# Turning the second 128 tokens inside the product ahead of it, eps on VectorE, and a closing product in quarters

## The chip, the cores and the metric

The kernel runs on one core of a Trainium2 chip. TensorE multiplies matrices, VectorE, ScalarE and POOL (GpSimd) work elementwise, and SP (SyncE) issues most of the DMAs. Each engine has its own queue and takes its instructions in the order in which they are written; it waits at the head of the queue until what the instruction needs is there. The metric is the device time of one execution in microseconds (us), as the median of several runs. Before the change it is 985.27 us (three runs, 982.47 to 986.35).

## The reference

A trunk of two layers works on 256 tokens of 1024 numbers each. A layer has three sub-layers, and each ends in a layer norm:

```python
for i in range(DEPTH):
    h = _layernorm(DN_ALPHA * h + 0.5 * _swiglu(h, ffn_w_in[i, 0], ffn_w_out[i, 0]), ln_g[i, 0], ln_b[i, 0])
    ...  # mix = _s5_mixer(h) in layer 0, _gmlp_mixer(h) in layer 1
    h = _layernorm(DN_ALPHA * h + mix, ln_g[i, 1], ln_b[i, 1])
    h = _layernorm(DN_ALPHA * h + 0.5 * _swiglu(h, ffn_w_in[i, 1], ffn_w_out[i, 1]), ln_g[i, 2], ln_b[i, 2])

def _swiglu(x, w_in, w_out):
    gate, up = jnp.split(x @ w_in, 2, axis=-1)
    return (jax.nn.silu(gate) * up) @ w_out
```

The SwiGLU has an inner width of 2816. The gMLP mixer starts with `gelu(x @ w_in + b_in)`, splits it into `u` and `v`, and normalises `v`. The norm is `(y - mean) * rsqrt(var + 1e-5) * g + b` over the 1024 numbers of a token.

## The kernel before

**Tiles.** The 256 tokens are two tiles of 128, `h[0]` and `h[1]` (t = 0 and 1), one token per partition. A product needs the tokens turned, features on partitions: `make_xt(t)` (L195) turns one tile with 8 small matmuls against the identity (`tps`, L187). ScalarE then writes the high part `xt` (L192) and VectorE the remainder (L193), in two halves of 512 columns. Every matrix product is done as three matmuls of such parts, high by high, high by low and low by high (`mm3`, L200: lines 201 to 203; `mm3t`, L205: lines 208 to 210).

**Weights.** `Stream` brings the weights in blocks of 128 x 2048 numbers. SP loads a block into one of three raw slots (L63), ScalarE casts it to `hi` and VectorE subtracts to `lo` (L88 and L89, or L96 and L97). At most five split blocks are alive. A block is split when `ws.tick(n)` is called at its place in the program, up to n blocks, and a raw slot is loaded anew once VectorE's subtraction has read it. So the places of the ticks set where the casts and subtractions stand in the queues of ScalarE and VectorE.

**A sub-layer boundary.** `close` (L276) ends a sub-layer: for t = 0 and then t = 1 it sums the last weight blocks into `acc`. Each tile's layer norm follows on VectorE: `r` (L239), statistics (L240, L247), two subtractions (L228), two final passes (L231). Its `rstd` comes from POOL in two instructions (`rstd_of`, L219): eps is added (L221), then the power -1/2 is taken (L222). Within the sums of t = 1, `close` turns `h[0]`. The next sub-layer then begins with t = 0: in an FFN with `step_in(0, 0)` and `step_in(1, 0)` (L361), the first two chunks of 256 inner columns, each a product of 24 matmuls of 512 columns; in the gMLP with `step_v` (L535) in the same way. Then `make_xt(1)` turns `h[1]`, and `step_in(0, 1)` and `step_in(1, 1)` follow for t = 1.

**What follows a step.** `in_act` (L354) applies silu on ScalarE and multiplies on VectorE (`g`, tile `sgg`, L358). In the steps for t = 1, `finish_g` (L343) transposes, after the first half of the product, the `g` that stand waiting (L348), at the first such place those of `step_in(0, 0)` and `step_in(1, 0)` together. Each step calls `ws.tick()` twice, in its middle and at its end. In the gMLP the additions of the bias to `v` (L547) and the norm of `v` follow the first two steps, and then eight heads of `u` (`step_u`, L550), 24 matmuls of 256 columns each.

**The boundaries here.** Three FFNs begin in this way (at about 341, 531 and 795 us of the profile), and the gMLP once (at 722 us). The first FFN and the S5 mixer begin in other ways.

**The end.** The last `close` sums the closing three blocks of the last FFN: for each t 18 matmuls for columns 0 to 511 and 18 for columns 512 to 1023 (`mm_out`, L441). The two halves of each normalised tile go out by one DMA each, from SP and from ScalarE's queue.

Of the kernel before, what the change touches and what calls it, by code (L numbers as in the profile page):

```python
# [9 lines left out]
F32 = mybir.dt.float32  # L10
# [3 lines left out]
ALU = mybir.AluOpType  # L14
PSUM = bass.MemoryType.PSUM

P = 128
D = 1024
KD = D // P
# [3 lines left out]
NCH = DFF // FC  # L23
# [131 lines left out]
def hybrid(ctx: ExitStack, tc: tile.TileContext, a: dict, out: bass.AP, subs=SUBS):  # L155
    nc = tc.nc
# [62 lines left out]
    def rstd_of(mv, eps):  # L219
        rstd = st_p.tile([P, 2], F32, tag="rstd", name="rstd")  # L220
        nc.gpsimd.tensor_scalar(rstd[:, 0:1], mv[:, 1:2], eps, 1.0, op0=ALU.add, op1=ALU.mult)  # L221
        nc.gpsimd.tensor_tensor(rstd[:, 1:2], rstd[:, 0:1], mhalf, op=ALU.pow)  # L222
        return rstd[:, 1:2]
# [51 lines left out]

    def close(li, si, acc, blocks, mm, gb, hscale, eps, last):  # L276

        order = [(n, j) for n in range(2) for j in range(len(blocks))]
        for t in range(2):
            for n, j in order:  # L280
                for kt in range(2):
                    mm(j, t, n, kt, acc[t][n])
                    if (t, n, j, kt) == (1, 1, len(blocks) - 2, 0) and not last:
# [7 lines left out]
            if t == 1 and not last:  # L291
                ws.tick(1)
            layernorm(t, acc[t], gb, hscale, eps, sums)
            if t == 1 and not last and next_kind[li, si] != "s5":
                ws.tick(1, 4)
            if last:
                for n in range(2):
                    s = slice(512 * n, 512 * n + 512)
                    (nc.sync, nc.scalar)[n].dma_start(out=out[0, P * t:P * t + P, s], in_=h[t][:, s])
# [33 lines left out]
    def ffn(ids, li, si, first, last):  # L333
        acc = [None, None]
        gts = {}
        pend = []
# [104 lines left out]
        def mm_out(c, t, n, kt, ps):  # L441
            gh, gl = (gts[c, kt][:, j, P * t:P * t + P] for j in range(2))
            wh, wl = ws.get(ids["out"][c])
            s = slice(D * kt + 512 * n, D * kt + 512 * n + 512)
            mm3(ps, gh, gl, wh[:, s], wl[:, s], c == 0 and kt == 0, c == NCH - 1 and kt == 1)
# [34 lines left out]
        close(li, si, acc, [ids["out"][c] for c in range(c0, NCH)], lambda j, t, n, kt, ps: mm_out(c0 + j, t, n, kt, ps),  # L480
# [48 lines left out]
    def gmlp(plan, par, pool, li, si, first, last):  # L529
# [5 lines left out]
        def step_v(c, t):  # L535
            ps = mm_p.tile([P, 512], F32, tag="mm", name="zps")
            in_mm(cols[c], t, ps, range(4))
            ws.tick()
            in_mm(cols[c], t, ps, range(4, KD))
            if t == 1:  # L540
                done(cols[c])
            ws.tick()
# [48 lines left out]
        pend = [step_v(0, 0), step_v(1, 0)]  # L591
        make_xt(1)
# [751 lines left out]
```

## Time and profile before

| | before |
|---|---|
| median of three runs | 985.27 us (982.47 to 986.35) |
| the profiled execution | 983.81 us, of which its span is 981.7 us |
| TensorE busy with matmuls | 948.4 us (97%) |
| VectorE busy | 650.1 us (66%) |
| ScalarE busy | 425.9 us (43%) |
| POOL busy | 165.6 us (17%) |
| mean granted clock of TensorE | 0.990 |
| chain of work that ended last | TensorE 66%, VectorE 18%, DMA 6%, POOL 3% |

The span is the time from the first to the last instruction of the profiled execution; the execution's own time is 2.1 us longer. Matmuls overlap, so their step from one start to the next is the measure of what they cost, not their duration. The chain follows the work that ended last back through the whole execution. In its second half it runs through TensorE alone, except at the sub-layer boundaries, where it passes through VectorE's norm.

### The profile page before, as it was taken

How to read it: one execution, taken by the hardware profiler on the slowest of the kernel's cores; microseconds unless marked ns; L12 is line 12 of the kernel's file. 1: busy time of each engine (PE TensorE's matmuls, PEld its weight loads, DVE VectorE, ACT ScalarE, POOL GpSimd, SP SyncE). 2: the span in 40 equal slices, each digit the busy share in tenths (PEclk: the TensorE clock that was granted, in tenths of full speed). 3: DMA queues.
4: the chain of work that ended last, by engine and by line, in shares of the span. 5: the costliest groups of instructions: out<-in, count | busy, mean ns of one | idle time of the engine just before them, and what ended most of it. 6: DMA issues, size and time to landing. Idle time of an engine off the chain costs nothing.

```text
span 981.7 us, 16616 instructions
## 1 busy us (share of the span) xinstructions
PE 948.4 (97%) x6988; PEld 860.6 (88%) x6988; DVE 650.1 (66%) x801; ACT 425.9 (43%) x504; POOL 165.6 (17%) x249
## 2 busy tenths in 40 slices
PE   7997999999999999999999999999999999999996
PEld 5996989978887789999997999999879879999995
DVE  5858999778797955455467644536588766453635
ACT  5554355644335445343423634344345445433430
POOL 1868811001572100000002000000011010000001
PEclk9998999999899999999999999999999999999998
DMA  8874796968645665746466674655447457555521
GB/s 278 224 223 162 265 280 220 289 214 285 221 146 183 189 209 179 237 133 233 152 200 216 211 272 154 204 182 179 164 155 275 129 173 265 163 194 192 168 90 43
DMA packets 133354, 195.10 MB, mean 199 GB/s; under 512 B 7120, under 2 KB 103936, under 8 KB 133280
## 3 DMA queue, kind: packets, MB, share of 16 engines
q1 hardware_dynamic: 128432, 182.34, 56.0%
q0 software_dynamic: 4560, 11.19, 3.9%
q8 instruction: 54, 0.88, 0.4%
q10 hardware_dynamic: 288, 0.52, 0.1%
q14 instruction: 20, 0.16, 0.0%
HBM read 184.07 MB, written 9.96 MB: 198 GB/s over the span
## 4 chain that ended last, share of the span: by engine, by line
PE 66%; DVE 18%; DMA 6%; POOL 3%; issue 3%; ACT 2%; SPq 0%; POOLq 0%; DVEq 0%; ACTq 0%
PE ips L210 11%; PE ips L209 11%; PE ips L208 11%; PE acc L201 7%; PE acc L202 7%; PE acc L203 7%; DVE lo L89 4%; DVE lo L97 4%; PE pps L1075 2%; DVE pq L639 1%; PE ips L203 1%; DMA raw<-in_ffn_w_out 1%; DVE prod L639 1%; ACT hi L96 1%; PE ips L201 1%
## 5 line engine op out<-in xcount | busy, mean ns | idle before, releaser
L210 PE MATMUL ips<-xt,lo 128*128 128x256 f32 x1184 | 335.5, 283 | 2.8 <-DVE lo L89 2.2
L208 PE MATMUL ips<-xt,hi 128*128 128x256 f32 x1184 | 335.4, 283 | 0.0
L209 PE MATMUL ips<-xt,hi 128*128 128x256 f32 x1184 | 335.0, 283 | 0.0
L89 DVE TENSOR_TENSOR lo<-raw,hi 128x2048 fp32r<-128x2048 f32 x107 | 242.9, 2292 | 11.1 <-ACT hi L88 10.7
L210 PEld LDWEIGHTS ips<-xt,lo 128*128 128x128 f32 x1184 | 227.1, 192 | 3.6 <-DVE lo L89 2.8
L208 PEld LDWEIGHTS ips<-xt,hi 128*128 128x128 f32 x1184 | 227.1, 192 | 1.5
L209 PEld LDWEIGHTS ips<-xt,hi 128*128 128x128 f32 x1184 | 227.1, 192 | 1.4
L88 ACT CAST hi<-raw 128x2048 fp32r<-128x2048 f32 x107 | 204.1, 1909 | 47.2 <-PE acc L203 26.6
L202 PE MATMUL acc<-lo,gt 128*128 128x512 f32 x352 | 138.5, 393 | 6.6 <-DVE lo L89 6.6
L398 DVE TENSOR_TENSOR sgg<-ips,sgg 128x256 f32<-128x256 f32 x74 | 31.3, 423 | 163.9 <-ACT sgg L397 163.8
L201 PE MATMUL acc<-hi,gt 128*128 128x512 f32 x352 | 138.7, 394 | 0.6 <-ACT gt L406 0.5
L203 PE MATMUL acc<-hi,gt 128*128 128x512 f32 x352 | 137.8, 391 | 0.0
L397 ACT ACTIVATE sgg<-ips 128x256 f32<-128x256 f32 x74 | 28.3, 383 | 214.2 <-PE ips L210 213.0
L221 POOL TENSOR_SCALAR rstd<-mv 128x1 f32<-128x1 f32 x14 | 10.4, 741 | 636.8 <-DVE mv L247 613.0
L97 DVE TENSOR_TENSOR lo<-raw,hi 128x2048 fp32r<-128x2048 f32 (+2 forms) x52 | 89.6, 1754 | 22.6 <-ACT hi L96 22.4
L202 PEld LDWEIGHTS acc<-lo,gt 128*128 128x128 f32 x352 | 66.7, 189 | 20.0 <-DVE lo L89 7.5
L201 PEld LDWEIGHTS acc<-hi,gt 128*128 128x128 f32 x352 | 66.7, 189 | 14.2 <-ACT gt L406 1.3
L203 PEld LDWEIGHTS acc<-hi,gt 128*128 128x128 f32 x352 | 66.5, 189 | 14.3 <-DVE gt L407 0.3
L96 ACT CAST hi<-raw 128x2048 fp32r<-128x2048 f32 (+2 forms) x52 | 74.5, 1482 | 3.6 <-DMA raw<-in_ffn_w_in 2.9
L407 DVE TENSOR_TENSOR gt<-sgg,gt 128x256 fp32r<-128x256 f32 x74 | 31.3, 423 | 59.5 <-ACT gt L406 59.5
L406 ACT CAST gt<-sgg 128x256 fp32r<-128x256 f32 x74 | 30.1, 406 | 68.1 <-DVE sgg L398 67.9
L201 PE MATMUL ips<-hi,xt 128*128 128x512 f32 x112 | 44.9, 401 | 3.8 <-ACT xt L192 2.3
(230 smaller groups left out, 1227.0 us busy)
## 6 DMA issues: line engine op xcount, KB each, us to landing
raw<-in_ffn_w_in SPq DMA_DIRECT2D x172, 512.0 KB, 5.8
raw<-in_ffn_w_out SPq DMA_DIRECT2D x44, 1024.0 KB, 5.2
raw<-in_g_w_in SPq DMA_DIRECT2D x8, 1024.0 KB, 5.8
rows<-w SPq DMA_DIRECT2D x8, 512.0 KB, 3.8
raw<-in_s_w_in SPq DMA_DIRECT2D x4, 1024.0 KB, 7.2
raw<-in_s_w_glu SPq DMA_DIRECT2D x4, 1024.0 KB, 5.2
w<-rows SPq DMA_DIRECT2D x8, 512.0 KB, 5.3
tc<-tc SPq DMA_DIRECT2D x16, 256.0 KB, 5.4
```

Of the source, the lines that this page charges most:

```text
L88: nc.scalar.copy(hi, raw)
L89: self.unfinished.append(lambda: nc.vector.tensor_tensor(lo, raw, hi.bitcast(F32), op=ALU.subtract))
L96: nc.scalar.copy(hi[:, s], raw[:, s])
L97: eng[p % len(eng)].tensor_tensor(lo[:, s], raw[:, s], hi[:, s].bitcast(F32), op=ALU.subtract)
L201: nc.tensor.matmul(ps, xh, wh, start=start, stop=False)
L202: nc.tensor.matmul(ps, xh, wl, start=False, stop=False)
L203: nc.tensor.matmul(ps, xl, wh, start=False, stop=stop)
L208: nc.tensor.matmul(ps, wh, xh, start=start, stop=False)
L209: nc.tensor.matmul(ps, wh, xl, start=False, stop=False)
L210: nc.tensor.matmul(ps, wl, xh, start=False, stop=stop)
L398: nc.vector.tensor_tensor(g, ps[:, 1], sg, op=ALU.mult)
L407: nc.vector.tensor_tensor(x[:, 1], g, x[:, 0].bitcast(F32), op=ALU.subtract)
```

## The change

The change has three parts.

**The turn.** `make_xt(1)` is called within `step_in(1, 0)` and `step_v(1, 0)`, after five of its eight k instead of after the whole step. The steps for (0, 0) no longer split a block (`split=0`); the first split after the boundary now stands behind the turn.

**eps.** `rstd_of` adds eps on VectorE; POOL keeps the power.

**The end.** `close_last` replaces `close` for the last FFN. For t = 1, columns 512 to 1023, the sum of the earlier blocks is closed early (`end` in `mm_out`) and added to `r` ahead of time. The last three blocks are summed for 256 columns at a time in tiles of their own (`ops`). Statistics are taken per 256 columns for t = 1, and the final pass and the output are in three parts, 512, 256 and 256 columns.

```diff
     def rstd_of(mv, eps):
         rstd = st_p.tile([P, 2], F32, tag="rstd", name="rstd")
-        nc.gpsimd.tensor_scalar(rstd[:, 0:1], mv[:, 1:2], eps, 1.0, op0=ALU.add, op1=ALU.mult)
+        nc.vector.tensor_scalar(rstd[:, 0:1], mv[:, 1:2], eps, 1.0, op0=ALU.add, op1=ALU.mult)
...
+    def close_last(acc, blocks, mm, gb, hscale, eps):
+        for t in range(2):
+            r = ln_p.tile([P, D], F32, tag="r", name="r", bufs=2)
+            parts = [(0, 512), (512, 512)] if t == 0 else [(0, 512), (512, 256), (768, 256)]
+            step = parts[-1][1]
+            st = st_p.tile([P, D // step, 6], F32, tag="bst", name="bst")
+            if t == 1:
+                s = slice(512, D)
+                nc.vector.scalar_tensor_tensor(r[:, s], in0=h[t][:, s], scalar=hscale, in1=acc[t][1], op0=ALU.mult, op1=ALU.add)
+            for i, (c, w) in enumerate(parts):
+                s, n = slice(c, c + w), c // 512
+                ps = acc[t][n] if w == 512 else mm_p.tile([P, 512], F32, tag="mm", name="ops")[:, 0:w]
+                for j in range(len(blocks)):
+                    for kt in range(2):
+                        mm(j, t, n, kt, ps, (c % 512, w), w < 512 and j == 0 and kt == 0)
...
+                x, scale = (h[t], hscale) if w == 512 else (r, 1.0)
+                nc.vector.scalar_tensor_tensor(r[:, s], in0=x[:, s], scalar=scale, in1=ps, op0=ALU.mult, op1=ALU.add)
+                for x in range(c, c + w, step):
+                    nc.vector.bn_stats(st[:, x // step], r[:, x:x + step])
...
+            for i, (c, w) in enumerate(parts):
+                s = slice(c, c + w)
+                nc.vector.scalar_tensor_tensor(h[t][:, s], in0=r[:, s], scalar=rstd, in1=b[:, s], op0=ALU.mult, op1=ALU.add)
+                (nc.sync, nc.scalar)[i % 2].dma_start(out=out[0, P * t:P * t + P, s], in_=h[t][:, s])
...
-        def step_in(c, t):
+        def step_in(c, t, mid=None, split=1):
             ps = mm_p.tile([P, 512], F32, tag="mm", name="ips")
-            in_mm(ids["in"][c], t, ps, range(4))
+            cut = 5 if mid else 4
+            in_mm(ids["in"][c], t, ps, range(cut))
+            if mid:
+                mid()
             if t:
                 finish_g()
-            ws.tick()
-            in_mm(ids["in"][c], t, ps, range(4, KD))
+            ws.tick(split)
+            in_mm(ids["in"][c], t, ps, range(cut, KD))
             in_act(c, t, ps)
             if t == 1:
                 done(ids["in"][c])
-            ws.tick()
+            ws.tick(split)
...
-            step_in(0, 0)
-            step_in(1, 0)
-            make_xt(1)
+            step_in(0, 0, split=0)
+            step_in(1, 0, lambda: make_xt(1))
             step_in(0, 1)
             step_in(1, 1)
...
-        pend = [step_v(0, 0), step_v(1, 0)]
-        make_xt(1)
+        pend = [step_v(0, 0, split=0), step_v(1, 0, lambda: make_xt(1))]
```

`step_v` is changed in the same way as `step_in`.

How this moves the instructions is shown at three places. A row names a line, an operation, what it writes and reads, and how often it stands there.

The first place is the beginning of the last FFN. This is a piece of the difference on TensorE. `tps` is the turn of `h[1]` (`h_95`); the weights `hi_7792` and `lo_7793` are the second half of `step_in(1, 0)`, `hi_7655` the beginning of `step_in(0, 1)`.

```order
@@ -4672,4 +4672,5 @@
 L202 MATMUL ips<-lo_7793,xt 128x512
 L203 MATMUL ips<-hi_7792,xt 128x512
+L187 MATMUL tps<-ident,h_95 128x128 x8
 L201 MATMUL ips<-hi_7792,xt 128x512
 L202 MATMUL ips<-lo_7793,xt 128x512
@@ -4681,5 +4682,4 @@
 L202 MATMUL ips<-lo_7793,xt 128x512
 L203 MATMUL ips<-hi_7792,xt 128x512
-L187 MATMUL tps<-ident,h_95 128x128 x8
 L201 MATMUL ips<-hi_7655,xt 128x512
 L202 MATMUL ips<-lo_7656,xt 128x512
```

The turn has moved up by nine matmuls. On VectorE there stood at the same place before the change (`lo` is a block split, `sgg` the `g` of a step, `xt` the turned tokens, `gt` the transposed `g`):

```order
L97 TENSOR_TENSOR lo_7793<-raw_7659,hi_7792 128x512 x4
L97 TENSOR_TENSOR lo_7819<-raw_7672,hi_7818 128x2048
L358 TENSOR_TENSOR sgg<-ips,sgg 128x256 x2
L193 TENSOR_TENSOR xt<-tps,xt 128x512 x2
L352 TENSOR_TENSOR gt<-tps,gt 128x128 x4
```

and now there stands on VectorE:

```order
L97 TENSOR_TENSOR lo_7793<-raw_7659,hi_7792 128x512 x4
L392 TENSOR_TENSOR sgg<-ips,sgg 128x256
L193 TENSOR_TENSOR xt<-tps,xt 128x512 x2
L97 TENSOR_TENSOR lo_7864<-raw_7672,hi_7863 128x2048
L392 TENSOR_TENSOR sgg<-ips,sgg 128x256
L386 TENSOR_TENSOR gt<-tps,gt 128x128 x4
```

The subtraction of the whole block (128x2048) has moved behind the turned tokens, and the second `g` behind that. ScalarE's cast of this block and its two silus have moved in the same way.

The second place is the beginning of the gMLP. VectorE before (`v` is the addition of the bias, BN_STATS the statistics of its norm):

```order
L97 TENSOR_TENSOR lo_7129<-raw_6998,hi_7128 128x512 x4
L97 TENSOR_TENSOR lo_7164<-raw_7010,hi_7163 128x2048
L193 TENSOR_TENSOR xt<-tps,xt 128x512 x2
L547 TENSOR_TENSOR v_7140<-zps,b_v 128x512 x2
L566 BN_STATS bst<-v_7140 128x6 x2
```

VectorE now:

```order
L97 TENSOR_TENSOR lo_7129<-raw_6998,hi_7128 128x512 x4
L193 TENSOR_TENSOR xt<-tps,xt 128x512 x2
L97 TENSOR_TENSOR lo_7206<-raw_7010,hi_7205 128x2048
L587 TENSOR_TENSOR v_7140<-zps,b_v 128x512 x2
L606 BN_STATS bst<-v_7140 128x6 x2
```

The block now stands between the turned tokens and the additions to `v`.

The third place is the end of the program, the norm of the last tile on VectorE. Before:

```order
L239 SCALAR_TENSOR_TENSOR r<-h_95,acc 128x512
L240 BN_STATS bst<-r 128x6
L239 SCALAR_TENSOR_TENSOR r<-h_95,acc 128x512
L240 BN_STATS bst<-r 128x6
L247 BN_AGGR mv<-bst 128x2
L228 SCALAR_TENSOR_TENSOR r<-r,mv,gam 128x512 x2
L231 SCALAR_TENSOR_TENSOR h_95<-r,rstd,bet 128x512 x2
```

Now:

```order
L286 SCALAR_TENSOR_TENSOR r<-h_95,acc 128x512
L298 SCALAR_TENSOR_TENSOR r<-h_95,acc 128x512
L300 BN_STATS bst<-r 128x6 x2
L298 SCALAR_TENSOR_TENSOR r<-r,ops 128x256
L300 BN_STATS bst<-r 128x6
L298 SCALAR_TENSOR_TENSOR r<-r,ops 128x256
L300 BN_STATS bst<-r 128x6
L302 BN_AGGR mv<-bst 128x2
L221 TENSOR_SCALAR rstd<-mv 128x1
L306 SCALAR_TENSOR_TENSOR r<-r,mv,gam 128x512 x2
L309 SCALAR_TENSOR_TENSOR h_95<-r,rstd,bet 128x512
L309 SCALAR_TENSOR_TENSOR h_95<-r,rstd,bet 128x256 x2
```

What waits for the last matmul is now 256 columns wide, and eps (`TENSOR_SCALAR rstd`) has come between the aggregation and the subtractions.

## Rows read from the trace of the kernel before

**Rows 1.** the page, part 1: busy us (share of the span), instructions; TensorE

```profile
PE 948.4 (97%) x6988; PEld 860.6 (88%) x6988; DVE 650.1 (66%) x801; ACT 425.9 (43%) x504; POOL 165.6 (17%) x249
```

**Rows 2.** TensorE's waits: who waited for whom, us in total, times, longest

```profile
PE ips L201 <- ACT xt L192: 2.3, 3, 0.8
...
PE tps L187 <- DVE h L231: 1.6, 2, 0.8
```

**Rows 3.** timeline, TensorE, last FFN's beginning: start, us, line, operation [idle before <- releaser]

```profile
792.60 0.39 PE L201 MATMUL ips<-hi,xt 128*128 128x512 f32 x1
...
793.45 0.40 PE L201 MATMUL ips<-hi,xt 128*128 128x512 f32 x1
...
795.50 1.03 PE L187 MATMUL tps<-ident,h 128*128 128x128 f32 x8
...
798.48 0.40 PE L201 MATMUL ips<-hi,xt 128*128 128x512 f32 x1
...
800.54 0.60 PE L348 MATMUL tps<-ident,sgg 128*128 128x128 f32 x4
```

**Rows 4.** timeline, TensorE, the gMLP's beginning, with the turn in `close` ahead

```profile
708.13 1.03 PE L187 MATMUL tps<-ident,h 128*128 128x128 f32 x8
...
709.23 0.39 PE L202 MATMUL acc<-lo,gt 128*128 128x512 f32 x1
...
722.14 1.03 PE L187 MATMUL tps<-ident,h 128*128 128x128 f32 x8
...
724.93 0.40 PE L201 MATMUL zps<-hi,xt 128*128 128x512 f32 x1
...
735.16 0.28 PE L208 MATMUL zps<-xt,hi 128*128 128x256 f32 x1
...
737.92 0.28 PE L210 MATMUL zps<-xt,lo 128*128 128x256 f32 x1
```

**Rows 5.** timeline, ScalarE, there

```profile
708.76 1.08 ACT L192 CAST xt<-tps 128x512 fp32r<-128x512 f32 x2 [9.78 <-PE tps L187]
```

**Rows 6.** timeline, VectorE, last FFN's beginning

```profile
792.13 4.69 DVE L97 TENSOR_TENSOR lo<-raw,hi 128x512 fp32r<-128x512 f32 x5
796.74 0.75 DVE L358 TENSOR_TENSOR sgg<-ips,sgg 128x256 f32<-128x256 f32 x2
```

**Rows 7.** the page, parts 5 and 6: groups (busy, mean ns), DMA issues (landing)

```profile
L89 DVE TENSOR_TENSOR lo<-raw,hi 128x2048 fp32r<-128x2048 f32 x107 | 242.9, 2292 | 11.1 <-ACT hi L88 10.7
...
L88 ACT CAST hi<-raw 128x2048 fp32r<-128x2048 f32 x107 | 204.1, 1909 | 47.2 <-PE acc L203 26.6
...
raw<-in_ffn_w_in SPq DMA_DIRECT2D x172, 512.0 KB, 5.8
```

**Rows 8.** timeline, VectorE, the gMLP's beginning

```profile
724.60 1.28 DVE L547 TENSOR_TENSOR v<-zps,b_v 128x512 f32<-128x512 f32 x2
...
740.53 0.68 DVE L547 TENSOR_TENSOR v<-zps,b_v 128x512 f32<-128x512 f32 x1
```

**Rows 9.** timeline, VectorE, the end of the program

```profile
973.52 0.69 DVE L239 SCALAR_TENSOR_TENSOR r<-h,acc 128x512 f32<-128x512 f32 x1 [1.85 <-PE acc L203]
...
974.97 0.21 DVE L247 BATCH_NORM_AGGREGATE mv<-bst 128x2 f32<-128x12 f32 x1
975.21 1.41 DVE L228 SCALAR_TENSOR_TENSOR r<-r,mv,gam 128x512 f32<-128x512 f32 x2
977.07 1.41 DVE L231 SCALAR_TENSOR_TENSOR h<-r,rstd,bet 128x512 f32<-128x512 f32 x2 [0.44 <-POOL rstd L222]
```

**Rows 10.** timeline, POOL, the end of the program

```profile
976.10 0.94 POOL L222 TENSOR_TENSOR rstd<-rstd,mhalf 128x1 f32<-128x1 f32 x1
```

**Rows 11.** groups of VectorE by line and shape: a narrow TENSOR_SCALAR

```profile
L645 DVE TENSOR_SCALAR n<-ch 128x32 f32<-128x32 f32 x1 | 0.2, 172 | 0.0
```

**Rows 12.** timeline, SP's DMA issues, last FFN's beginning

```profile
796.85 12.59 SPq L63 DMA_DIRECT2D raw<-in_ffn_w_in  x4
```

**Rows 13.** timeline, ScalarE, there

```profile
810.97 1.91 ACT L96 CAST hi<-raw 128x2048 fp32r<-128x2048 f32 x1
```

More of the change, by code (lines that the diff above doesn't have):

```diff
@@ L274, in new_acc @@
         return [acc_p.tile([P, 512], F32, tag="acc", name="acc") for _ in range(2)]
+    def close_last(acc, blocks, mm, gb, hscale, eps):
[13 more added lines that the diff above has]
+                        mm(j, t, n, kt, ps, (c % 512, w), w < 512 and j == 0 and kt == 0)
+                    if t == 0 and i == 0 and j < 2:
+                        ws.tick()
+                    if (t, i) == (1, len(parts) - 1):
+                        ws.done(blocks[j])
+                x, scale = (h[t], hscale) if w == 512 else (r, 1.0)
+                nc.vector.scalar_tensor_tensor(r[:, s], in0=x[:, s], scalar=scale, in1=ps, op0=ALU.mult, op1=ALU.add)
+                for x in range(c, c + w, step):
+                    nc.vector.bn_stats(st[:, x // step], r[:, x:x + step])
+            mv = st_p.tile([P, 2], F32, tag="mv", name="mv")
+            nc.vector.bn_aggr(mv, st)
+            rstd, (g, b) = rstd_of(mv, eps), gb
+            for n in range(2):
+                s = slice(512 * n, 512 * n + 512)
+                nc.vector.scalar_tensor_tensor(r[:, s], in0=r[:, s], scalar=mv[:, 0:1], in1=g[:, s], op0=ALU.subtract, op1=ALU.mult)
+            for i, (c, w) in enumerate(parts):
+                s = slice(c, c + w)
+                nc.vector.scalar_tensor_tensor(h[t][:, s], in0=r[:, s], scalar=rstd, in1=b[:, s], op0=ALU.mult, op1=ALU.add)
+                (nc.sync, nc.scalar)[i % 2].dma_start(out=out[0, P * t:P * t + P, s], in_=h[t][:, s])
@@ L276, in close @@
     def close(li, si, acc, blocks, mm, gb, hscale, eps, last):
+        if last:
+            return close_last(acc, blocks, mm, gb, hscale, eps)
         order = [(n, j) for n in range(2) for j in range(len(blocks))]
@@ L282, in close @@
                     mm(j, t, n, kt, acc[t][n])
-                    if (t, n, j, kt) == (1, 1, len(blocks) - 2, 0) and not last:
+                    if (t, n, j, kt) == (1, 1, len(blocks) - 2, 0):
                         make_xt(0, next_kind[li, si] == "s5")
@@ L290, in close @@
                     sums = layernorm_half(t, acc[t][0], 0, hscale)
-            if t == 1 and not last:
+            if t == 1:
                 ws.tick(1)
             layernorm(t, acc[t], gb, hscale, eps, sums)
-            if t == 1 and not last and next_kind[li, si] != "s5":
+            if t == 1 and next_kind[li, si] != "s5":
                 ws.tick(1, 4)
[L296 to L299, printed above, removed]
     def plan_ffn(li, fi, fine):
@@ L439, in start_in, with mm_out @@
             done(ids["in"][0])
-        def mm_out(c, t, n, kt, ps):
+        def mm_out(c, t, n, kt, ps, cols=(0, 512), start=False):
             gh, gl = (gts[c, kt][:, j, P * t:P * t + P] for j in range(2))
             wh, wl = ws.get(ids["out"][c])
-            s = slice(D * kt + 512 * n, D * kt + 512 * n + 512)
-            mm3(ps, gh, gl, wh[:, s], wl[:, s], c == 0 and kt == 0, c == NCH - 1 and kt == 1)
+            s = slice(D * kt + 512 * n + cols[0], D * kt + 512 * n + sum(cols))
+            end = NCH - 4 if last and (t, n) == (1, 1) and cols[1] == 512 else NCH - 1
+            mm3(ps, gh, gl, wh[:, s], wl[:, s], start or c == 0 and kt == 0, c == end and kt == 1)
         def step_out(c, t):
@@ L479, in ffn @@
         c0 = NCH - 3
-        close(li, si, acc, [ids["out"][c] for c in range(c0, NCH)], lambda j, t, n, kt, ps: mm_out(c0 + j, t, n, kt, ps),
+        close(li, si, acc, [ids["out"][c] for c in range(c0, NCH)], lambda j, *args: mm_out(c0 + j, *args),
               gb, 2 * ALPHA, 4 * EPS, last)
@@ L533, in gmlp, with step_v @@
         u = [pool.tile([P, SEQ], F32, name=f"u{h}") for h in range(HEADS)]
-        def step_v(c, t):
+        def step_v(c, t, mid=None, split=1):
             ps = mm_p.tile([P, 512], F32, tag="mm", name="zps")
-            in_mm(cols[c], t, ps, range(4))
-            ws.tick()
-            in_mm(cols[c], t, ps, range(4, KD))
+            cut = 5 if mid else 4
+            in_mm(cols[c], t, ps, range(cut))
+            if mid:
+                mid()
+            ws.tick(split)
+            in_mm(cols[c], t, ps, range(cut, KD))
             if t == 1:
                 done(cols[c])
-            ws.tick()
+            ws.tick(split)
             return c, t, ps
```

## The prediction

> **What bounds the kernel now.** Read the busy times of the engines first: TensorE's matmuls fill 97% of the 981.7 us span [rows 1]. VectorE and ScalarE have slack on average, so an edit on them is worth only what TensorE waits for, plus what lies behind the last matmul. The second view is therefore the list of TensorE's waits [rows 2]. Two of its lines belong to this change: three waits for the copies of the turned tokens (`ips L201 <- ACT xt`, 2.3 us in all) and two for the normalised tokens themselves (`tps L187 <- DVE h`, 1.6 us). The third view is the timeline of one sub-layer boundary, from which each of these gets its true size: a wait that is cut in pieces by a matmul in between shows only its first piece in the list.
>
> **1. The turn of tokens 128–255 (`make_xt(1)`), at three FFN boundaries.** Today TensorE finishes the product `step_in(1, 0)`, turns `h[1]` with 8 small matmuls, and then needs the result at once. From the first of the 8 at 795.50 to the fourth matmul of the next product at 798.48 [rows 3] pass 2.98 us. Nine matmuls take 2.05 us (793.45 to 795.50, [rows 3]), so one is 0.228 and three are 0.68; the turn costs 2.30 us at this place. Where `close` turns the other tokens inside a product, the trace has the price of a turn with cover: from its first matmul at 708.13 to the second one behind it at 709.23 [rows 4], 1.10 less one matmul, 0.87 us. The change makes every such turn a covered one: nine matmuls (2.05 us) follow it before the copies are wanted. The copies need 0.63 us until ScalarE starts (708.13 to 708.76) and 1.08 us for both halves [rows 4, 5], 1.71 in all; VectorE's part follows each by about 0.6. TensorE comes to them 0.87 + 2.05 = 2.92 us after the turn began, so the wait goes: 2.30 − 0.87 = 1.43 us.
>
> A second piece comes off in front of it. The matmuls of k = 4 take 0.85 us instead of 0.68 (792.60 to 793.45, [rows 3]), because their `lo` piece leaves VectorE only then (its run begins at 792.13, [rows 6]). That run hangs on the layer norm, which part 3 shortens by 0.22 us. So 0.17 us more, 1.60 in all.
>
> What the move pushes back is the block split that stood ahead of the turn. On ScalarE and VectorE the cast and the subtraction of 128x2048 elements (1.91 and 2.29 us, [rows 7]) now stand behind the copies of the turn, and the product `g` of `step_in(1, 0)`, which VectorE did directly after that of `step_in(0, 0)`, stands behind the subtraction. `finish_g` transposes this `g` twelve matmuls into the next product (800.54 now, [rows 3]). From the start of the turn: 1.71 + 1.91 + 2.29 + 0.42 (one of the two at 796.74, 0.75 together, [rows 6]) = 6.33 us. TensorE comes there after 0.87 + 21 × 0.228 = 5.66, and 0.18 more for the first pair, which is ready: 5.84. **A new wait of 0.5 us.** Its bounds: 0.2 if the row-to-row overlaps of some 0.1 us each hold here, 1.0 if cast or subtraction starts late by as much. I take 0.5, the plain sum of rows. Net 1.60 − 0.5 = 1.1 us, three times: **3.3 us**.
>
> **2. The same turn ahead of the gMLP product.** From 722.14 to the fourth matmul at 724.93 [rows 4] pass 2.79 us; less 0.68 and 0.87, 1.24, and with the 0.17 in front **1.4 us**. Here nothing transposes a `g`; the delayed split delays the additions to `v`. VectorE reaches the first of them 5.91 us (1.71 + 1.91 + 2.29) after a turn that starts at 722.14 − 2.05 − 0.17 = 719.92, so at 725.8 instead of 724.60 [rows 8]: 1.2 later. Its chain stays in that order until the last addition (740.53, 0.68 us, [rows 8]), then at about 741.5 to 742.2, as the norm between them gives 0.22 back. TensorE wants the bank that this frees for the fourth head: heads start at 735.16, are 24 matmuls of 0.12 us (23 of them between 735.16 and 737.92, [rows 4]), so at 735.16 − 1.4 + 3 × 2.88 = 742.4. That is cover of 0.2 us; if it is gone, it costs some tenths.
>
> **3. eps on VectorE instead of POOL.** In each of 14 norms VectorE waits for `rstd` (0.44 us at the last, [rows 9]), since POOL first adds eps and then takes the power (0.94 us, [rows 10]). Now VectorE adds, and POOL's power runs under the two subtractions: 0.94 us against 977.07 − 975.21 − 0.44 = 1.42 us [rows 9]. The wait goes and a one-column instruction comes. The trace has none on VectorE. Its bounds are 0.17 us (32 columns, [rows 11]) and 0.24 us, the step from the 12-column aggregation to what waits for it (974.97 to 975.21, [rows 9]); zero is excluded, since the addition must end before POOL starts and VectorE is in order. I take 0.22, so 0.22 us gained per norm. [...] On the path this lies only where TensorE waits for `h`: the two turns of [rows 2], **0.4 us** together, and the tail. Elsewhere matmuls hide it.
>
> **4. The tail.** The last 512 columns are summed as 18 + 18 matmuls of 256 columns instead of 18 of 512. TensorE: 36 × 0.12 against 18 × 0.228 is 0.22 later, about the same until the result can be read. VectorE then has half the columns for sum and statistics: from 973.52 to 974.97 [rows 9] are 1.45 us, two instructions of 0.42 with 0.03 between are 0.90, so −0.55; the earlier part's additional instructions run while TensorE still computes. eps +0.22, the wait for `rstd` −0.44, the last pass in three parts +0.1 (one more fixed part, estimated from 0.42 for 256 columns against 1.41 for two of 512, [rows 6, 9]). Sum: 0.22 − 0.55 + 0.22 − 0.44 + 0.1 = **−0.45 us**. What follows (981.7 − 978.5 = 3.2 us for the last output DMA and its end) I leave as it is, although the last transfer is half as large; at best that is some tenths more. [...]
>
> **Sum.** 3.3 + 1.4 + 0.4 + 0.45 = 5.6 us. Against the profiled execution's own 983.8 us this gives 978.2. The three timed runs (982.5, 985.3, 986.4) and it have their middle at 984.5, a little under the stated median of 985.27; from there 978.9, said as 979.0.
>
> **Rivals.** *The wait moves instead of going.* The transposes of `g` wait for a split that was hidden until now. If ScalarE's cast or VectorE's subtraction comes a microsecond late, each FFN boundary nets 0.1 instead of 1.1, and the time is 984.5 − 2.6 = 981.9. For it: 0.5 us of this wait stands in the sum already. Against it: both blocks have landed long before, and both engines are idle there.
>
> [...]
>
> *Slower: the weight stream falls behind.* SP's queue keeps its order, but the raw slot of the moved split is refilled only when its subtraction is over. Now that is 796.8 [rows 12]; then 793.3 + 5.9 = 799.2, while TensorE is 1.1 ahead: 3.4 us later against TensorE. A stream without slack would hand this over at all four boundaries, 13.6 − 5.6 = 8 us, 992.5. Against it: the load issued at 796.85 lands in 5.8 us [rows 7] and is first cast at 810.97 [rows 13]. That is 8.3 us of slack, of which 4.9 remain; it decides from a landing of 10.7 us on.
>
> **How the numbers follow.** Forecast 0.56, moved wait 0.25, hardly any new wait 0.15, slower 0.04. A measurement of this kernel can tell 0.5% (4.9 us, 980.3) from no change. Single runs of before lie 4 us apart, so I let a quarter of the forecast fall short of that line, and nearly all of the moved wait: faster 0.61, same 0.34, slower 0.05. The range goes from the better case with a low base (976) to the moved wait with a high one (983).
>
> **What would show it.** Right: no `ACT xt` or `DVE xt` wait among TensorE's longest after 330 us; in its place three of about 0.5 us of the transposes of `sgg` for VectorE; 9 matmuls between turn and next product without a gap; no idle time before the `rstd` pass; about 0.9 us between the last matmul's result and the aggregation. Wrong: waits over 1 us at the `sgg` transposes or at the heads of the gMLP, VectorE's one-column instruction over 0.44 us, or TensorE waiting for `lo` within the two chunks that follow a boundary.

## The result and the profile after

The changed kernel takes 977.83 us as the median of 13 runs (975.61 to 982.53), beside 984.23 for 13 runs of the kernel before (981.69 to 986.35). The ratio is 0.9936 with a 95% interval of 0.9921 to 0.9952: 6.3 us, or 0.64%, faster. The profiled execution took 976.03 us, its span is 974.3.

The engines' busy times (page, part 1; columns as in [rows 1]) have hardly changed, and so the gain is waiting time:

```profile
PE 948.1 (97%) x7006; PEld 863.4 (89%) x7006; DVE 652.0 (67%) x820; ACT 425.4 (44%) x504; POOL 157.2 (16%) x235
```

TensorE's waits (us in total, times, longest). Before, the list had for the gMLP, beside the lines of [rows 2],

```profile
PE zps L201 <- DVE xt L193: 1.0, 1, 1.0
```

After, neither this line nor that of `ACT xt` is on the list any more; the wait for `h` of [rows 2] fell from 1.6 to 0.6, and the new wait for the second `g` has come:

```profile
PE tps L382 <- DVE sgg L392: 0.6, 3, 0.2
PE tps L187 <- DVE h L231: 0.6, 2, 0.3
```

The beginning of the last FFN after, on TensorE, which answers to [rows 3] (start, us, line, operation, idle before and its releaser):

```profile
787.61 1.03 PE L187 MATMUL tps<-ident,h 128*128 128x128 f32 x8
788.40 0.48 PE L201 MATMUL ips<-hi,xt 128*128 128x512 f32 x1
788.72 0.40 PE L202 MATMUL ips<-lo,xt 128*128 128x512 f32 x1
...
790.54 0.39 PE L201 MATMUL ips<-hi,xt 128*128 128x512 f32 x1
...
793.27 0.38 PE L382 MATMUL tps<-ident,sgg 128*128 128x128 f32 x2
793.84 0.44 PE L382 MATMUL tps<-ident,sgg 128*128 128x128 f32 x2 [0.20 <-DVE sgg L392]
...
794.36 0.39 PE L202 MATMUL ips<-lo,xt 128*128 128x512 f32 x1
```

The turn at 787.61 is followed by nine matmuls without a gap, and the next product starts at 790.54 without a wait. The transposes of the first `g` start at 793.27, those of the second only at 793.84. From the first transpose to the second matmul behind them pass 1.09 us; before, the four together took 0.67, from 800.54 [rows 3] to the second matmul behind them,

```profile
801.21 0.39 PE L202 MATMUL ips<-lo,xt 128*128 128x512 f32 x1
```

So the new wait costs 0.42, of which the list shows 0.20. VectorE after shows why:

```profile
788.40 0.42 DVE L392 TENSOR_TENSOR sgg<-ips,sgg 128x256 f32<-128x256 f32 x1
788.87 1.29 DVE L193 TENSOR_TENSOR xt<-tps,xt 128x512 fp32r<-128x512 f32 x2
791.16 2.29 DVE L97 TENSOR_TENSOR lo<-raw,hi 128x2048 fp32r<-128x2048 f32 x1 [1.01 <-ACT hi L96]
793.37 0.42 DVE L392 TENSOR_TENSOR sgg<-ips,sgg 128x256 f32<-128x256 f32 x1
```

The second `g` (793.37) stands behind the block (791.16), as the order said, and is done at 793.79, 0.05 before TensorE goes on.

**Where the time went, place by place.** Take the same matmul in both traces and subtract its starts; where this shift grows, the change gains. Over the first FFN boundary, for example, these are the two matmuls before the change

```profile
335.10 0.39 PE L203 MATMUL ips<-hi,xt 128*128 128x512 f32 x1
...
518.22 0.48 PE L201 MATMUL acc<-hi,gt 128*128 128x512 f32 x1
```

and the same two after it:

```profile
333.22 0.39 PE L203 MATMUL ips<-hi,xt 128*128 128x512 f32 x1
...
515.15 0.48 PE L201 MATMUL acc<-hi,gt 128*128 128x512 f32 x1
```

The shift grows from 1.88 to 3.07 us, so this boundary gains 1.19. In the same way for all places, and for the experiments below (us gained against before; the pairs of matmuls start before the change at 213.09 and 219.21, 318.00 and 335.10, 335.10 and 518.22, 526.04 and 700.19, 716.06 and 782.29, 791.01 and 955.05; the end runs from 968.10 to the end of the span):

| kernel | turn that waits for `h`, first / second | FFN 1 / 2 / 3 | gMLP | end | sum |
|---|---|---|---|---|---|
| predicted | 0.2 / 0.2 | 1.1 / 1.1 / 1.1 | 1.4 | 0.45 | 5.6 |
| changed kernel | 0.48 / 0.53 | 1.19 / 1.16 / 1.14 | 1.42 | 0.64 | 6.56 |
| changed, second time | 0.47 / 0.52 | 1.19 / 1.14 / 1.18 | 1.42 | 0.64 | 6.56 |
| turn alone | −0.01 / 0.03 | 1.05 / 0.96 / 0.96 | 1.21 | 0.01 | 4.21 |
| eps alone | 0.48 / 0.52 | 0.47 / 0.46 / 0.47 | 0.19 | 0.49 | 3.08 |
| end alone | −0.01 / 0.04 | 0.03 / −0.06 / 0.00 | 0.00 | 0.16 | 0.16 |
| split left ahead | 0.47 / 0.50 | 0.83 / 0.73 / 0.82 | 0.49 | 0.63 | 4.47 |
| split behind, turn not moved (FFN) | 0.46 / 0.52 | 0.79 / 0.77 / 0.77 | 1.41 | 0.63 | 5.35 |
| split one product later | 0.49 / 0.53 | 0.80 / 0.78 / 0.77 | 1.42 | 0.63 | 5.42 |
| turn after four k | 0.58 / 0.52 | 1.62 / 1.54 / 1.60 | 1.42 | 0.64 | 7.92 |
| transposes later | 0.46 / 0.53 | 1.62 / 1.55 / 1.60 | 1.43 | 0.64 | 7.83 |
| transposes later, second time | 1.14 / 0.48 | 1.62 / 1.54 / 1.60 | 1.43 | 0.62 | 8.43 |

The two spans differ by 7.45 us, 0.89 more than this sum. The rest lies in the first 213 us and in the S5 mixer, where the change touches nothing that TensorE waits for. When the changed kernel ran a second time, the sum was again 6.56, while the rest was −2.94 us. So a single span tells a part of this size poorly, and the places behind 318 us tell it to some hundredths. The first turn is less safe: in the last row it gained 1.14 instead of 0.46 to 0.58. There the list of waits has `h` once, with 0.3 us, where the changed kernel's two traces have it twice, with 0.6 in all; the mean granted clock from 205 to 320 us was 0.96 in that trace and 0.97 in the changed kernel's two. Why the first turn didn't wait there is not shown.

### The profile page after: what moved, and what is told of

Same layout as the page of the kernel before. It is cut to its first block, busy times and chain, and to the rows that moved or that the text cites. A ratio compares the mean times of both kernels' runs of the same rounds, so it can differ in the third digit from the quotient of the medians.

```text
span 974.3 us, 16658 instructions
## 1 busy us (share of the span) xinstructions
PE 948.1 (97%) x7006; PEld 863.4 (89%) x7006; DVE 652.0 (67%) x820; ACT 425.4 (44%) x504; POOL 157.2 (16%) x235
## 4 chain that ended last, share of the span: by engine, by line
PE 64%; DVE 1%; ACT 1%; issue 0%; DVEq 0%
PE ips L210 11%; PE ips L209 11%; PE ips L208 11%; PE acc L201 7%; PE acc L202 7%; PE acc L203 7%; PE ips L203 2%; PE ips L201 2%; PE ips L202 2%; PE zps L210 1%; PE zps L209 1%; PE zps L208 1%; PE zps L202 1%; PE zps L203 1%; PE zps L201 1%; DVE lo L97 1%
## 5 line engine op out<-in xcount | busy, mean ns | idle before, releaser
L202 PE MATMUL acc<-lo,gt 128*128 128x512 f32 x346 | 136.2, 394 | 4.4 <-DVE lo L89 4.4
L201 PE MATMUL acc<-hi,gt 128*128 128x512 f32 x346 | 136.2, 394 | 0.0
L203 PE MATMUL acc<-hi,gt 128*128 128x512 f32 x346 | 135.2, 391 | 0.0
L222 POOL TENSOR_TENSOR rstd<-rstd,mhalf 128x1 f32<-128x1 f32 x14 | 13.3, 951 | 640.8 <-DVE rstd L221 640.8
L203 PEld LDWEIGHTS acc<-hi,gt 128*128 128x128 f32 x346 | 65.4, 189 | 14.0 <-DVE gt L444 0.2
L201 PEld LDWEIGHTS acc<-hi,gt 128*128 128x128 f32 x346 | 65.4, 189 | 13.0 <-ACT gt L443 0.4
```

What stands on the lines that cost most here:

```text
L201: nc.tensor.matmul(ps, xh, wh, start=start, stop=False)
L202: nc.tensor.matmul(ps, xh, wl, start=False, stop=False)
L203: nc.tensor.matmul(ps, xl, wh, start=False, stop=stop)
```

## The experiments

**The three parts apart.** The theory was that the parts add up, each worth what the start-to-start times say. The first kernel has the turn (and the splits that it takes along) alone:

```diff
-            step_in(0, 0)
-            step_in(1, 0)
-            make_xt(1)
+            step_in(0, 0, split=0)
+            step_in(1, 0, lambda: make_xt(1))
```

> Only the turn of the tokens is moved (with the splits that it takes along); eps stays on POOL and the end stays as before. Theory (the parts add up, and each is worth what the start-to-start times of TensorE show): at each FFN boundary the stall of 1.43 us goes and a wait of 0.42 us for the second g comes, the gMLP boundary gains 1.27, so 3 x 1.01 + 1.27 = 4.3 us, about 980 from a base of 984.2; the pause of 0.17 us in k = 4 stays, since the layer norm is as slow as before. Rival (eps is what lets the turn pay, because the copies hang on the norm): under 3 us, and a wait of the copies of the turned tokens stays in TensorE's list. Rival (the wait moves): about 1 us, with waits of 1 us and more at the transposes of g.

Measured: 980.34 us (11 runs, 975.38 to 981.79), ratio 0.9952 (0.9935 to 0.9969); in the trace 4.21 us. No wait of the copies is left; two lines of TensorE's waits:

```profile
PE tps L187 <- DVE h L231: 1.6, 2, 0.8
...
PE tps L348 <- DVE sgg L358: 0.5, 3, 0.2
```

The theory holds, and the turn doesn't need the faster norm. The wait for `h` stands as in [rows 2]; the next kernel, with eps alone, must take it.

```diff
-        nc.gpsimd.tensor_scalar(rstd[:, 0:1], mv[:, 1:2], eps, 1.0, op0=ALU.add, op1=ALU.mult)
+        nc.vector.tensor_scalar(rstd[:, 0:1], mv[:, 1:2], eps, 1.0, op0=ALU.add, op1=ALU.mult)
```

> Only eps moves to VectorE. Theory (start to start): a norm is 0.49 us shorter, because the wait for rstd cost 0.56 from start to start and not the 0.44 that the trace calls idle, and because the one-column instruction holds VectorE up by 0.07 and not 0.22. On the path at the two turns that wait for h (0.98), in the tail (0.49) and in the four pauses of 0.17 us in k = 4 after a boundary: 2.1 us, about 982. Rival (the prediction's sizes, 0.22 per norm): 0.44 + 0.22 + 4 x 0.17 = 1.3 us. Rival (hidden everywhere but in the tail): 0.5 us.

Measured: 980.36 us (12 runs, 978.24 to 984.86), ratio 0.9971 (0.9956 to 0.9986); in the trace 3.08 us, more than any of the cases expected. The two turns and the end came out as the theory said (0.48, 0.52, 0.49). What it missed is 0.47 at each FFN boundary instead of 0.17. TensorE there:

```profile
791.88 1.03 PE L187 MATMUL tps<-ident,h 128*128 128x128 f32 x8
793.39 0.47 PE L201 MATMUL ips<-hi,xt 128*128 128x512 f32 x1 [0.48 <-DVE sgg L358]
...
794.56 0.40 PE L201 MATMUL ips<-hi,xt 128*128 128x512 f32 x1
```

and VectorE:

```profile
790.62 2.29 DVE L97 TENSOR_TENSOR lo<-raw,hi 128x2048 fp32r<-128x2048 f32 x1
792.82 0.75 DVE L358 TENSOR_TENSOR sgg<-ips,sgg 128x256 f32<-128x256 f32 x2
```

With the norm 0.49 shorter, the stall at the turn is 0.30 shorter too (794.56 − 791.88 = 2.68, against 2.98 before [rows 3]), and its releaser is now named as the first `g`: that is done at 792.82 + 0.42 = 793.24, and the matmul starts 0.15 later. Before, the first of the two `g` at 796.74 [rows 6] was done at 797.16, and the matmul started at 797.30, also 0.14 later, though the list put that wait down to ScalarE's copies. These are TensorE's rows of before, and VectorE's copies of the turned tokens behind its two `g`:

```profile
797.30 0.47 PE L201 MATMUL ips<-hi,xt 128*128 128x512 f32 x1 [0.77 <-ACT xt L192]
...
798.14 0.50 PE L203 MATMUL ips<-hi,xt 128*128 128x512 f32 x1
```

```profile
797.41 1.28 DVE L193 TENSOR_TENSOR xt<-tps,xt 128x512 fp32r<-128x512 f32 x2
```

So the stall that the change removes hung on VectorE's queue. The next product is taken to need the PSUM tile of the first one (the fourth tile before it in a pool of four), which is free when the first `g` has read it, and that `g` stood behind the block. Which tile it takes is read from the code; what the traces show is the same lag in both kernels. And this is only the first piece of the stall: the third matmul (798.14) waits once more, for VectorE's copy of the first half of the turned tokens, the remainder. This copy ends at 797.41 + 0.68 = 798.09, 0.05 before the matmul, and stands behind the block and both `g`: it began 0.69 after ScalarE's part was done (796.72), where 0.03 is enough in the split-behind kernel below. This was a new theory, and the next experiments are made for it.

The third part alone:

```diff
+        if last:
+            return close_last(acc, blocks, mm, gb, hscale, eps)
```

> Only the closing product is changed; eps stays on POOL. Theory: TensorE 0.22 later, 0.53 less between result and aggregation, 0.06 more for the aggregation of four parts, 0.13 more for a third final pass, the last store as slow as before: 0.1 to 0.2 us faster in the trace from the first matmul of the last 512 columns to the end, nothing that the times can tell. The wait for rstd of 0.44 us must still stand there. [...] Rival (the additional 18 matmuls cost more than the halves give): 0.2 us slower.

Measured: 985.86 us (12 runs, 982.71 to 990.46), ratio 1.0017 (0.9998 to 1.0036), which tells nothing from no change; in the trace 0.16 us. VectorE's last instructions:

```profile
973.37 0.42 DVE L298 SCALAR_TENSOR_TENSOR r<-r,ops 128x256 f32<-128x256 f32 x1 [0.64 <-PE ops L203]
...
974.29 0.26 DVE L302 BATCH_NORM_AGGREGATE mv<-bst 128x2 f32<-128x24 f32 x1
...
976.45 1.54 DVE L309 SCALAR_TENSOR_TENSOR h<-r,rstd,bet 128x512 f32<-128x512 f32 x3 [0.45 <-POOL rstd L222]
```

The result is aggregated 0.92 us after VectorE can read it (1.45 before, [rows 9]), the wait for `rstd` is still there, and what follows the last pass is 981.2 − 977.99 = 3.2 us as before. So the new end is worth about 0.15 us by itself, with eps (0.64 against 0.49 for eps alone) or without (0.16).

The three sums make 7.45 us (by chance as much as the two spans differ), the three together 6.56. The 0.89 between are gained twice: at the three FFN boundaries, the stall that eps shortens by 0.30 is the one that the turn's move removes.

**Turn or split?** The move of the turn took the block split along. Two kernels take them apart. In one the turn is moved and the split stays ahead of it:

```diff
-            step_in(0, 0, split=0)
+            step_in(0, 0)
...
-        pend = [step_v(0, 0, split=0), step_v(1, 0, lambda: make_xt(1))]
+        pend = [step_v(0, 0), step_v(1, 0, lambda: make_xt(1))]
```

> The changed kernel, but with the block split left ahead of the turn, where it stood before. Theory: the wait of 0.42 us for the second g goes from the three FFN boundaries; in its place VectorE comes to the copies of the turned tokens only after the block (2.29 us) and the first g, about 0.7 us after TensorE wants their low part, and in the gMLP about 0.3 after: 3 x 0.3 + 0.3 = 1.2 us slower than the changed kernel, with a new line of TensorE waiting for DVE xt. Rival (the move of the split was not needed, VectorE has room ahead of the turn): 1.2 us faster than the changed kernel.

Measured: 979.81 us (12 runs, 976.07 to 984.13), ratio 0.9963 (0.9945 to 0.9981); in the trace 2.1 us less gained than by the changed kernel, where 1.2 was expected. At the FFN the new wait is not that of the copies; TensorE, and then VectorE:

```profile
795.93 0.47 PE L201 MATMUL ips<-hi,xt 128*128 128x512 f32 x1 [0.47 <-ACT sgg L391]
```

```profile
795.37 0.42 DVE L392 TENSOR_TENSOR sgg<-ips,sgg 128x256 f32<-128x256 f32 x1
```

Again the product starts 0.14 after the first `g` is done (795.79), though the row names ScalarE. In the gMLP, which has no `g`, it is the copies, and the gain falls from 1.42 to 0.49:

```profile
723.23 0.50 PE L201 MATMUL zps<-hi,xt 128*128 128x512 f32 x1 [0.64 <-DVE xt L193]
```

In the other the turn is back behind the whole product, in the FFNs alone, and the split stands behind it:

```diff
-            step_in(1, 0, lambda: make_xt(1))
+            step_in(1, 0, split=0)
+            make_xt(1)
+            ws.tick()
```

> In the FFNs the turn is put back behind the whole product, and only the block split is taken from ahead of it: it now stands behind the turn. All else (gMLP, eps, end) is as in the changed kernel. Theory (what held the next product up was VectorE's queue, the block and the first g that frees the bank, as much as the turn itself): from the turn's first matmul to the fourth of the next product pass 2.06 us instead of 2.98, so the turn costs 1.38 instead of 2.30, against 0.88 inside the product; the second g comes before the block, so its wait of 0.42 does not exist. Each FFN boundary gains 1.0 to 1.1 us, nearly what the changed kernel gains (1.16): within 0.5 us of it in the sum. Rival (the prediction's reason, the place of the turn): the stall of 1.43 us stays, each boundary gains 0.2 to 0.5, and the kernel is 2 to 3 us slower than the changed one.

Measured: 980.22 us (12 runs, 974.83 to 983.15), ratio 0.9952 (0.9933 to 0.9971); each FFN boundary gains 0.78, between the theory and its rival. TensorE:

```profile
794.25 1.04 PE L187 MATMUL tps<-ident,h 128*128 128x128 f32 x8
795.53 0.50 PE L201 MATMUL ips<-hi,xt 128*128 128x512 f32 x1 [0.24 <-ACT xt L192]
...
796.25 0.50 PE L203 MATMUL ips<-hi,xt 128*128 128x512 f32 x1
796.59 0.40 PE L201 MATMUL ips<-hi,xt 128*128 128x512 f32 x1
```

ScalarE's copies and VectorE's:

```profile
794.89 1.07 ACT L192 CAST xt<-tps 128x512 fp32r<-128x512 f32 x2
```

```profile
795.50 1.29 DVE L193 TENSOR_TENSOR xt<-tps,xt 128x512 fp32r<-128x512 f32 x2 [0.21 <-ACT xt L192]
```

From the turn to the fourth matmul pass 2.34 us, 0.64 less than the 2.98 before. This is the queue's part of the stall. eps, which this kernel has too, takes 0.30 of it by itself (2.68 with eps alone); the other 0.34 is what the split's place takes here. The split's place without eps was not tried. The expected 2.06 was missed because the third matmul (796.25) still waits for VectorE's copy (795.50 + 0.69 = 796.19). That is the latency of the turn itself: ScalarE's copies start 0.64 after the turn, as they do inside the product (0.63), and VectorE's begin as soon as ScalarE's first is done. The place of the turn is worth the 0.78 that remain to the 0.88 of a covered turn. So both halves of the move were needed. With eps in all of them, the boundary gains 0.47 without either half (eps alone), about 0.8 with either one, and 1.16 with both.

**The new wait.** Three kernels change what the second `g` waits for. One lets TensorE ask later:

```diff
-            cut = 5 if mid else 4
+            cut = 5 if mid else cut
...
-            step_in(0, 1)
+            step_in(0, 1, cut=6)
```

> The changed kernel with the transposes of the first two g moved from behind k = 3 to behind k = 5 of the product for t = 1, six matmuls (1.36 us) later. Theory: the second g is ready 0.4 us after TensorE wanted it, so the wait goes whole: 0.42 us at each of three boundaries, 1.2 us faster than the changed kernel, each FFN boundary gains 1.6 against before. Rival (the wait moves on to the copies gt, or to the first product of the output): less than 0.5 us, with a new wait for gt in TensorE's list.

Measured: 976.93 us (6 runs, 973.44 to 979.86), ratio 0.9921 (0.9894 to 0.9948). Each FFN boundary gains 1.6, as expected. VectorE and TensorE:

```profile
791.15 0.42 DVE L392 TENSOR_TENSOR sgg<-ips,sgg 128x256 f32<-128x256 f32 x1
```

```profile
792.41 0.60 PE L382 MATMUL tps<-ident,sgg 128*128 128x128 f32 x4
```

The `g` is done at 791.57, the transposes want it at 792.41, all four in one go. The second kernel makes the `g` earlier, with the turn after four of eight k:

```diff
-            cut = 5 if mid else 4
+            cut = 4
```

> The changed kernel with the turn after four of the eight k instead of five, three matmuls (0.68 us) earlier. Theory: the chain copies, cast, block, second g hangs on the turn and comes 0.68 us earlier, which is more than the wait of 0.42: 1.2 us faster than the changed kernel, as by moving the transposes. Rival (the copies of the turned tokens on VectorE can not come earlier, as they stand behind the four pieces of lo and the first g): the block waits for ScalarE's cast only, so this would show as the block starting when VectorE is done with the copies; still no wait. Rival (the norm of the second tile is not ready): TensorE waits for h up to 0.5 us at each boundary, no gain or a loss.

Measured: 977.70 us (6 runs, 974.83 to 978.39), ratio 0.9927 (0.9905 to 0.9949), and the same 1.6 at each boundary; the norm of the second tile was ready in time. The third moves the split itself on, into the first product for t = 1:

```diff
-            step_in(1, 0, lambda: make_xt(1))
+            step_in(1, 0, lambda: make_xt(1), split=0)
```

> The changed kernel with the block's split taken out of the second product of the FFN too: it stands in the first product for t = 1, behind the transposes of g, about 6 us later than in the changed kernel. Theory (the weight stream has slack): the wait for the second g goes, 1.2 us faster than the changed kernel; the raw slot is loaded anew some 6 us later, which uses up the 4.8 us between landing and first cast and makes that cast up to 1.5 us late, but TensorE needs that block only later, so no wait of it for lo follows. Rival (the prediction's slower case, the stream has no slack left): each late microsecond is handed on, waits for lo in the chunks after a boundary, 1.3 us and more each, so 2 to 5 us slower than the changed kernel.

Measured: 979.93 us (12 runs, 973.82 to 984.28), ratio 0.9959 (0.9937 to 0.9980), 0.4 less at each boundary than the changed kernel. Neither case had it. The wait has moved one `g` on; VectorE, and the transposes on TensorE:

```profile
799.09 2.29 DVE L97 TENSOR_TENSOR lo<-raw,hi 128x2048 fp32r<-128x2048 f32 x1 [1.52 <-ACT hi L96]
801.29 0.42 DVE L392 TENSOR_TENSOR sgg<-ips,sgg 128x256 f32<-128x256 f32 x1
```

```profile
801.77 0.44 PE L382 MATMUL tps<-ident,sgg 128*128 128x128 f32 x2 [0.58 <-DVE sgg L392]
```

The weight stream did as the theory said. ScalarE's casts wait longer for the late loads: two of them here, 0.42 us (at 806.92) and 1.47,

```profile
810.30 1.91 ACT L88 CAST hi<-raw 128x2048 fp32r<-128x2048 f32 x1 [1.47 <-DMA raw<-in_ffn_w_in]
```

where in the changed kernel one waits 1.10 (at 807.13). But TensorE doesn't: from 330 to 960 us its list of waits has a single line, without any `lo`, as in the changed kernel, where this line is 0.6 us:

```profile
PE tps L382 <- DVE sgg L392: 1.7, 3, 0.6
```

**The size of a one-column instruction.** In each norm 16 more of them stand behind eps, eight that read the same aggregate, and eight in a chain:

```diff
+        for i in range(8):
+            nc.vector.tensor_scalar(one[:, i:i + 1], mv[:, 1:2], eps, 1.0, op0=ALU.add, op1=ALU.mult)
+        for i in range(8):
+            x = seq[:, i - 1:i] if i else mv[:, 1:2]
+            nc.vector.tensor_scalar(seq[:, i:i + 1], x, eps, 1.0, op0=ALU.add, op1=ALU.mult)
```

> The changed kernel with 16 more one-column additions on VectorE in each norm, behind the addition of eps: eight that read the aggregate and are independent, then eight of which each reads the one before. Nothing uses their results. Theory (a one-column instruction lasts 0.15 us but its successor starts after 0.07 when it does not need the result): eight independent ones take 8 x 0.07 = 0.55 us from the first start to the first of the chain; the chain takes 0.15 to 0.24 each, 1.2 to 1.9 us. Rival (the sizes of the prediction): 0.17 to 0.22 each in both, 1.4 to 1.8 us for the independent ones too. POOL's 0.94 us stays hidden in either case.

One run, 994.31 us, for its trace on VectorE:

```profile
785.84 0.57 DVE L226 TENSOR_SCALAR one<-mv 128x1 f32<-128x1 f32 x8
786.32 0.14 DVE L229 TENSOR_SCALAR seq<-mv 128x1 f32<-128x1 f32 x1
786.50 1.28 DVE L229 TENSOR_SCALAR seq<-seq 128x1 f32<-128x1 f32 x7
787.69 1.40 DVE L235 SCALAR_TENSOR_TENSOR r<-r,mv,gam 128x512 f32<-128x512 f32 x2
```

Eight independent ones take 786.32 − 785.84 = 0.48 us, 0.06 each. Seven of the chain take 787.69 − 786.50 = 1.19; the step from the last of them to the subtraction, which doesn't need its result, is 0.07, so six steps take 1.12, 0.19 each. Each instruction lasts 0.14 to 0.15.

**The better version beside the changed kernel.** Both once more, on one chip:

> The changed kernel itself, unaltered, beside the next one on the same chip: ratio to before 0.9936 as before, FFN boundaries 1.16 us, gMLP 1.44, the two turns in the closing products 0.5 each, the end 0.64 (shifts of TensorE's starts against before). What its starts up to 205 us and those of the S5 mixer are shifted by should come out anew, since the change touches nothing there before the first norm's end: it was -1.3 and +0.4 us.

> The version with the transposes of the first two g six matmuls later, again, beside the changed kernel: each FFN boundary 1.58 us against before instead of 1.16, so 1.2 us faster than the changed kernel in the trace, and a ratio to before of about 0.992. Rival: the earlier median (1 us under the changed kernel) came from the first 320 us, which vary by 2 us from run to run; then the boundaries would show no difference now.

Measured: 979.76 us (9 runs, 974.23 to 981.53), ratio 0.9940 (0.9916 to 0.9964), and 976.86 us (6 runs, 973.17 to 980.47), ratio 0.9912 (0.9882 to 0.9943). In the trace the version with the later transposes gains 1.62, 1.54 and 1.60 at the FFN boundaries again, the changed kernel 1.19, 1.14 and 1.18. So 1.25 us of the sum is shown place by place and twice, and both pairs of medians have the same sign; the times of whole runs alone, which lie 4 to 10 us apart within one kernel, would not settle it.

## Why the prediction was right, and where it was not

The forecast was 979.0 us, within 976 to 983; measured were 977.8 and 979.8. By places it was 5.6 against 6.56 us.

**The turn at the FFN boundaries: the size was right, and half of the reason.** Predicted 1.1, measured 1.14 to 1.19. The covered turn cost 0.88 (788.72 − 787.61, less one matmul), predicted 0.87. The second `g` was to be there 6.33 us after the turn began; TensorE went on after 6.23, and the wait cost 0.42 instead of 0.5. But the step "TensorE then needs the result at once" took the stall for the turn's own latency, as the list of waits had it. About 0.64 of the 1.42 was VectorE's queue instead, the block and the two `g` ahead of its copies: that much less passes in the split-behind kernel, 0.30 of it through eps and 0.34 through the split's place. The split-ahead kernel shows that the turn's move without the split's gives 0.8 at an FFN, 0.47 of which eps gives alone, and in the gMLP 0.49 instead of 1.42. The diff did both at once, which is why the sum came out; that it came out with half of the reason missing was luck.

**The gMLP: right.** Predicted 1.4, measured 1.42. The last addition to `v` stands at 736.89 and lasts 0.68, and the fourth head starts at 738.11, so the cover was 0.5 and not 0.2. Here the stall before was the turn's own latency, as predicted: VectorE's first copy began at 723.39, just behind ScalarE's (done at 723.36), and the block ahead of it (to 723.46) held it up by next to nothing. The row of before:

```profile
723.39 1.29 DVE L193 TENSOR_TENSOR xt<-tps,xt 128x512 fp32r<-128x512 f32 x2
```

**eps: the mechanism was right, the term too small.** Predicted 0.22 per norm, measured 0.49. Two sizes failed in the step "the wait goes and a one-column instruction comes". The wait of 0.44 [rows 9] is the idle time that the trace shows; from start to start, the passes `L228` to `L231` took 1.86 us before (975.21 to 977.07) and take 1.32 now, so it was worth 0.54. And the new instruction holds VectorE up by 0.07, not 0.22, since the subtraction behind it doesn't need its result:

```profile
967.85 0.26 DVE L302 BATCH_NORM_AGGREGATE mv<-bst 128x2 f32<-128x24 f32 x1
968.15 0.15 DVE L221 TENSOR_SCALAR rstd<-mv 128x1 f32<-128x1 f32 x1
968.22 1.40 DVE L306 SCALAR_TENSOR_TENSOR r<-r,mv,gam 128x512 f32<-128x512 f32 x2
969.54 1.54 DVE L309 SCALAR_TENSOR_TENSOR h<-r,rstd,bet 128x512 f32<-128x512 f32 x3
```

The 0.24 taken from the aggregation was the step to an instruction that waits for it, the wrong neighbour. Nor is its duration what such an instruction costs here: one lasts 0.14 to 0.15, while the steps are 0.06 between independent ones and 0.19 in the chain.

**The tail: 0.64 instead of 0.45.** Term by term, from first matmul of the last 512 columns to the end: TensorE 0.22 later (962.43 to 966.93 now, 969.24 to 973.52 before), as predicted; result to aggregation 0.92 against 1.45, −0.53 (predicted −0.55); aggregation to subtraction 0.37 against 0.24, +0.13 (predicted +0.22; 0.06 of it is the aggregation of four parts); the wait −0.54 (−0.44); the third pass +0.13 (+0.1); behind the last pass 974.25 − 971.08 = 3.17 against 3.22, −0.05 (0). The error is eps again. The tenths that the prediction allowed at best for a last store of half the size are shown by no run: stores of 256 KB (before, the two from ScalarE's queue, as their median) and the last one of 128 KB (after, from SP's) land after the same 2.1 us:

```profile
out<-h ACTq DMA_DIRECT2D x2, 256.0 KB, 2.1
```

```profile
out<-h SPq DMA_DIRECT2D x1, 128.0 KB, 2.1
```

**The rivals.** "The wait moves" needed the block a microsecond late; ScalarE's cast began 1.60 us after the turn, against 1.71 in the sum. "Hardly any new wait" was wrong too: the wait cost 0.42, though the list shows 0.2. "The weight stream falls behind": SP's load was issued at 793.48, and where the split was moved by another product, two casts waited up to 1.5 us for their loads, and TensorE did not wait for `lo`. The delay that this rival names came, the loss did not.

## What to carry to other kernels

A wait in a profile names who came last, not everyone who would have come late: before a stall is costed, write down for each condition of the waiting instruction (its PSUM tile among them), and of the next two or three behind it, when it was met. Cost instructions from start to start and by the neighbour they have, and take parts apart by the starts of the same instruction in two traces, which shows hundredths where whole runs show microseconds. If work must be moved behind a deadline, look for the consumer that can be asked later: here six matmuls' delay of the four transposes brought 1.25 us on top of the 4.2 that the moved turn brings alone.

## What the runs showed of the hardware

- A one-column instruction on VectorE lasts 0.14 to 0.15 us; the next starts 0.06 to 0.08 after it when it is independent and 0.18 to 0.19 after it when it needs its result.
- Where the product for t = 1 fell behind VectorE's first `g`, its first matmul started 0.14 to 0.15 us after that instruction's end, three times in three kernels (797.30, 793.39, 795.93). The transposes that waited for the second `g` started 0.05 after its end (793.79 to 793.84), and so did the matmul that waited for VectorE's copy (798.09 to 798.14). Why the first lag is longer was not tried.
- The stores of 256 KB from ScalarE's queue (before, median of two) and the last one of 128 KB from SP's (after) landed 2.1 us after they were issued.
- Runs of equal code differ early. TensorE's matmuls of 512 columns stepped by 0.43 us where the granted clock was 0.50 (86 to 92.3 us before, 89 to 92.2 after), and by 0.23 where it was 1.00 (92.5 to 100 us in both traces). From 60 to 100 us the mean granted clock was 0.91 in the trace before and 0.96 in that after: behind a wait for `lo` (5.8 us before, 3.5 after), the step was 0.43 up to 92.3 us before and 92.2 after.
- The steps differ at the start too. The records of the granted clock begin at 10.5 us in the trace before and at 17.2 in that after, at 1.00 in both; ahead of the first record the views show 1.00 too. But after, the matmuls step by 0.43 from 13.3 to 17.1 us and by 0.23 from 17.4 on, while before they step by 0.23 from 12.2 on. So the steps of 0.43 went on longer there after the change; which clock was granted ahead of the first record is not shown. None of these stretches is near an edit, and it is in the first 320 us that two spans of the same kernel part.
